# Four edits to a two-layer transformer trunk: priority for the closings, remainder products last, epsilon on VectorE, both token blocks in one cast

## The chip, the core and the metric

The program runs on one core of a Trainium2 chip. The metric is the device time of one launch, in microseconds (us), as the median of three runs. Shares of the span are not the metric; they only help to find where the time is spent.

## What is computed

The reference is a trunk of two post-norm layers over 256 tokens of width 1024, float32. Layer 0 mixes tokens by causal softmax attention with 16 heads of 64, layer 1 by differential attention with 8 heads of 2 x 64; each mixer is followed by a squared-ReLU MLP of width 4096. Every sub-layer is modulated by vectors that come from a conditioning vector c and is closed by a LayerNorm:

```python
h = x * (1 + scale1) + shift1
y = mixer(h)                                    # moba_attention or diff_attention
x = layer_norm(ALPHA * x + (1 + gate1) * y, ln_g[i, 0], ln_b[i, 0])
h = x * (1 + scale2) + shift2
y = square(relu(h @ w_up[i])) @ w_down[i]
x = layer_norm(ALPHA * x + (1 + gate2) * y, ln_g[i, 1], ln_b[i, 1])
```

The modulation vectors are silu(c) @ ada_w + ada_b, six of 1024 for each layer. A LayerNorm divides by the root of its variance plus 1e-5, and differential attention has an RMS norm for each head with the same epsilon.

## The kernel before

**Tiles.** The 256 tokens are two blocks (b = 0, 1) of 128 partitions. Every product is made in float32 precision out of three rounded products: each operand is split into a rounded part `hi` (ScalarE casts it) and a remainder `lo` (VectorE subtracts), and TensorE adds hi x hi, hi x lo and lo x hi in one PSUM bank (`mm3`, L165 to L169, called by `dense`, L171; `dense2`, L176, is the form with two banks for products of width 1024). Weights come by DMA from SyncE's queue into three `raw` buffers and are split in pieces of 128 x 1024 (`split_piece`, L127: cast at L130, subtraction at L131) into 8 `hi` and 8 `lo` buffers. A product of one block with 512 columns and depth 1024 takes 24 matmuls and four such pieces.

**The first pass** (L494 to L541) makes the first columns of V, Q and K of layer 0. For each of 8 depth steps j it loads two blocks of ada_w and reduces them against silu(c) on VectorE (L216, names `aw`) to the scale and shift column `ab`, adds 1 to the scale (L499), loads 1536 columns of weights and splits them, transposes the tokens of both blocks, modulates both at once on ScalarE (L518), and then casts and subtracts block by block (L521, L522). 18 matmuls follow.

**The order of the work** after that is the list `PROGRAM` (L45): V and Q are products, T transposes, S, P, F attention, O the output product, B a boundary (waits for its gate vector, spreads it over the partitions), C a closing, U and X the up product and its transposes, D the down product, Y up products of both blocks together, E the last one. `f` takes steps from a queue of fillers: the other modulation vectors (L216 again, its tile named `aw`, loads in two buffers) and the residuals (L331, L332). In each layer C00 and C10 close the mixer, C01 and C11 the MLP.

**A closing** (`close`, L592) runs `layer_norm` (L280): on VectorE the gate times the accumulator (L289), the residual (L292), the statistics (L302) and their aggregate (L303); then `rsqrt_eps` (L276), on GpSimd, adds epsilon (L277) and raises to the power -0.5 (L278); VectorE normalizes the first half (L308) and makes the bias of the second (L310), which ScalarE normalizes (L311). `modulate` (L314) transposes on TensorE (L320), scales on ScalarE (L324), casts (L327) and subtracts on VectorE (L328) into the tiles `hT` that the next V or U product reads. The last closing (A is None, L594) writes the output and has no `modulate`. Differential attention calls `rsqrt_eps` too (L467), on the sums of L465, ahead of L468.

**Who sets each engine's order.** The instructions of an engine run in a fixed order that is made when the program is built: a list scheduler steps through an estimate of the execution and, whenever an engine comes free there, gives it the most urgent of the instructions that are ready. Urgency is the order in which the program was written; `tc.high_priority()` puts what stands in its block ahead. SyncE's queue, which issues the loads, is ordered in the same way.

```python
def rsqrt_eps(dst, src):
    pool_e.tensor_scalar(out=dst, in0=src, scalar1=EPS, scalar2=None, op0=ALU.add)
    pool_e.tensor_tensor(out=dst, in0=dst, in1=nhalf.to_broadcast(list(src.shape)), op=ALU.pow)
```

Of the kernel before, what the change touches and what calls it, by code (L numbers as in the profile page):

```python
# [16 lines left out]
F32 = mybir.dt.float32  # L17
F32R = mybir.dt.float32r
AF = mybir.ActivationFunctionType
ALU = mybir.AluOpType  # L20
AX = mybir.AxisListType

P = 128
D = 1024
S = 256
KC = D // P
# [6 lines left out]
EPS = 1e-5  # L33
# [33 lines left out]
SHIFT1, SCALE1, GATE1, SHIFT2, SCALE2, GATE2 = range(6)  # L67
# [5 lines left out]
def tile_trunk(ctx: ExitStack, tc: tile.TileContext, x, c, moba_w_in, moba_w_out, diff_w_in, diff_w_out,  # L73
               lam_q1, lam_k1, lam_q2, lam_k2, subln_g, ada_wt, ada_b, ln_g, ln_b, w_up, w_down, cst, out):
    nc = tc.nc
    vec, act, pe, pool_e, sp = nc.vector, nc.scalar, nc.tensor, nc.gpsimd, nc.sync
# [4 lines left out]
    ap_ = ctx.enter_context(tc.tile_pool(name="acts", bufs=1))  # L81
# [83 lines left out]
    def mm3(dst, lhs, rhs, start, stop):  # L165
        (xh, xl), (wh, wl) = lhs, rhs
        pe.matmul(dst, lhsT=xh, rhs=wh, start=start, stop=False)  # L167
        pe.matmul(dst, lhsT=xh, rhs=wl, start=False, stop=False)  # L168
        pe.matmul(dst, lhsT=xl, rhs=wh, start=False, stop=stop)  # L169

    def dense(dst, lhs, rhs):  # L171
        n = len(lhs)
        for k in range(n):
            mm3(dst, lhs[k], rhs[k], k == 0, k == n - 1)

    def dense2(dsts, lhs, rows, start, stop):  # L176

# [11 lines left out]
    tabT = cpool.tile([P, P], F32, name="tabT")  # L189
# [68 lines left out]
    def halves(t, b):  # L258

        return t[:, :, b * P:(b + 1) * P], t[:, :, (2 + b) * P:(3 + b) * P]  # L260
# [4 lines left out]
    def block_ops(tiles, b):  # L265
        return as_ops([halves(t, b) for t in tiles])
# [7 lines left out]
        return t  # L274

    def rsqrt_eps(dst, src):  # L276
        pool_e.tensor_scalar(out=dst, in0=src, scalar1=EPS, scalar2=None, op0=ALU.add)  # L277
        pool_e.tensor_tensor(out=dst, in0=dst, in1=nhalf.to_broadcast(list(src.shape)), op=ALU.pow)  # L278

    def layer_norm(b, accs, gate, parts=None):  # L280
# [33 lines left out]
    def modulate(b, z, A, B, tiles):  # L314
        for h in range(2):
            hi, lo = halves(tiles[h], b)
            ps = psum("tp")
            full = ap_.tile([P, 512], F32, tag="full", name="full", bufs=2)
            for k in range(4):
                pe.transpose(out=ps[:, k * P:(k + 1) * P], in_=z[:, (h * 4 + k) * P:(h * 4 + k + 1) * P], identity=ident)  # L320
            for k in range(4):
                j = h * 4 + k
                ks = slice(k * P, (k + 1) * P)
                act.activation(out=full[:, ks], in_=ps[:, ks], func=AF.Identity, scale=A[:, j:j + 1],  # L324
                               bias=B[:, j:j + 1])
            f3 = full.rearrange("p (k t) -> p k t", t=P)
            act.copy(out=hi, in_=f3)  # L327
            vec.tensor_tensor(out=lo, in0=f3, in1=hi, op=ALU.subtract)  # L328
# [161 lines left out]
    hT0 = act_tiles()  # L490
# [3 lines left out]
    def first_operand(j):  # L494

        ab = small.tile([P, 2], F32, tag="ab0", name="ab0", bufs=3)
        ada_rows(0, SCALE1, j, ab[:, 0:1], "bc", 3)
        ada_rows(0, SHIFT1, j, ab[:, 1:2], "aw", 2)
        vec.tensor_scalar(out=ab[:, 0:1], in0=ab[:, 0:1], scalar1=1.0, scalar2=None, op0=ALU.add)  # L499
        def load_x(cols):  # L500
            for b in range(2):
                sp.dma_start(out=xt[b][:, cols], in_=x[0, b * P:(b + 1) * P, cols])

        if j == 0:
            load_x(slice(0, 256))
        raw = raw_tile()
        wr = moba_w_in[0][j * P:(j + 1) * P, :]
        sp.dma_start(out=raw[:, 0:512], in_=wr[:, 2 * D:2 * D + 512])
        for s_ in range(2):
            sp.dma_start(out=raw[:, 512:1536].rearrange("p (g s n) -> p s g n", g=2, s=2)[:, s_],  # L510
                         in_=wr[:, s_ * D:s_ * D + 512].rearrange("p (g n) -> p g n", n=256))
        if j == 1:
            load_x(slice(256, D))
        tp = psum("tp")
        for b in range(2):
            pe.transpose(out=tp[:, b * P:(b + 1) * P], in_=xt[b][:, j * P:(j + 1) * P], identity=ident)
        full = ap_.tile([P, 512], F32, tag="full", name="full", bufs=2)
        act.activation(out=full[:, :256], in_=tp[:, :256], func=AF.Identity, scale=ab[:, 0:1], bias=ab[:, 1:2])  # L518
        for b in range(2):
            hi, lo = halves(hT0[j // 4], b)  # L520
            act.copy(out=hi[:, j % 4, :], in_=full[:, b * P:(b + 1) * P])  # L521
            vec.tensor_tensor(out=lo[:, j % 4, :], in0=full[:, b * P:(b + 1) * P], in1=hi[:, j % 4, :], op=ALU.subtract)  # L522
        h1, l1 = split_piece(raw[:, 0:1024])
        h2, l2 = split_piece(raw[:, 1024:1536], 512)
        return [(h1[:, 0:512], l1[:, 0:512]), (h1[:, 512:1024], l1[:, 512:1024]), (h2[:, 0:512], l2[:, 0:512])]
# [8 lines left out]
    tps = psum("tp")  # L534
    pe.transpose(out=tps[:, 0:P], in_=t1, identity=ident)
    vec.tensor_copy(out=tabT, in_=tps[:, 0:P])
    ws = first_operand(0)
    for j in range(KC):
        wn = first_operand(j + 1) if j + 1 < KC else None
# [29 lines left out]
        queue_vector(*key)  # L569


    def unit(w, hT):
        ps = psum("mm")
        dense(ps, hT, w)
        return ps

    def out_proj(dsts, g2, b, rows):
# [14 lines left out]
    def close(l, i, b, accs, bd, tiles):  # L592
        A, B, gate, gb, bb = bd
        if A is None:  # L594
            parts = ((0, 512), (512, 1024))
            z, mv, rs = layer_norm(b, accs, gate, parts)
            for c0, c1 in parts:
                vec.scalar_tensor_tensor(out=z[:, c0:c1], in0=z[:, c0:c1], scalar=mv[:, 0:1], in1=gb[:, c0:c1],
                                         op0=ALU.subtract, op1=ALU.mult)
            for c0, c1 in parts:  # L600
                vec.scalar_tensor_tensor(out=z[:, c0:c1], in0=z[:, c0:c1], scalar=rs, in1=bb[:, c0:c1],
                                         op0=ALU.mult, op1=ALU.add)
                sp.dma_start(out=out[0, b * P:(b + 1) * P, c0:c1], in_=z[:, c0:c1])
            return
        z = layer_norm(b, accs, gate)
        modulate(b, z, A, B, tiles)
        filler.appendleft(lambda: residual(b, z, gb, bb))

    def run(program, st):
# [9 lines left out]
    def step_v(st, b, g2):  # L619
        l = st["l"]  # L620
        if l == 0 and g2 == 0:
            ps = kacc[b][0]
        else:
            w = step_load(st, ("wv", l, g2), lambda: load_cols(w_ins[l], v_cols(g2)))
            ps = unit(w, block_ops(st["x"], b))
        evict_v(b, g2, ps)

    def step_qk(st, b, g):
# [25 lines left out]
    def step_up(st, b, j):  # L654
        l = st["l"]
        w = step_load(st, ("wu", l, j), lambda: load_cols(w_up[l], [(j * 512, 512)]))
        ps = psum("mm")
        dense(ps, block_ops(st["x"], b), w)
        r = ap_.tile([P, 512], F32, tag="nat", name="nat", bufs=3)
        act.activation(out=r, in_=ps, func=AF.Relu)  # L660
        act.activation(out=r, in_=r, func=AF.Square)
        st["r", b, j] = r
# [75 lines left out]
    st = {"x": hT0}  # L738
# [48 lines left out]
```

## Time and profile before

| | |
|---|---|
| runs, us | 645.58, 642.77, 645.11 (median 645.11) |
| the profiled execution, us | 644.11, its span 640.7 |
| TensorE busy, share of the span | 609.0 us, 95% |
| VectorE, ScalarE, GpSimd busy | 500.4, 377.6, 22.2 us |
| DMA | 158.23 MB, mean 247 GB/s |

The span goes from the first to the last instruction; the time of the execution also has what lies around it. TensorE's busy time is not its peak, since matmuls are pipelined; so the gaps in it count, and who ended them.

### The profile page before, as it was taken

Reading aid. Unit: us, or ns where it says so; the run is one execution under the profiler, and the core shown is the slowest. Engines: PE = TensorE matmul, PEld = TensorE weight load, DVE = VectorE, ACT = ScalarE, POOL = GpSimd, SP = SyncE. Lnnn points to the kernel's source line nnn. Section 1 sums busy time; section 2 is a strip of 40 time slices with the busy share of each in tenths; the row PEclk is TensorE's granted clock in tenths of the full one; section 3 lists DMA queues with packets and bytes.
Section 4 is the critical chain, followed back from the end, with each engine's and each line's share of the span. In section 5 each row is a group of like instructions: output and inputs, shape, how many; then the busy total and the mean of one; then the engine's idle time right before and its main releaser. Section 6 shows DMA issues by size and latency. Waiting matters only on the chain.

```text
span 640.7 us, 8768 instructions
## 1 busy us (share of the span) xinstructions
PE 609.0 (95%) x3140; PEld 499.6 (78%) x3140; DVE 500.4 (78%) x903; ACT 377.6 (59%) x699; POOL 22.2 (3%) x37
## 2 busy tenths in 40 slices
PE   4889999998999999999999999989999999999994
PEld 3667887886888888888877787767788888888883
DVE  5798998889978878888799989977984646465446
ACT  3448665657846545664477676765775556475530
POOL 0000000001000000000000010021100000000002
PEclk9999999999999999999999999999999999999998
DMA  8997998876689888989765967682663764746401
GB/s 292 406 322 279 313 325 286 288 250 227 215 309 343 308 313 330 326 294 338 268 231 188 337 229 263 232 289 68 208 218 109 259 225 143 255 133 213 182 0 66
DMA packets 65941, 158.23 MB, mean 247 GB/s; under 512 B 4041, under 2 KB 21098, under 8 KB 65898
## 3 DMA queue, kind: packets, MB, share of 16 engines
q1 hardware_dynamic: 65898, 157.68, 70.1%
q8 instruction: 24, 0.39, 0.2%
q14 instruction: 19, 0.16, 0.1%
HBM read 156.62 MB, written 1.05 MB: 246 GB/s over the span
## 4 chain that ended last, share of the span: by engine, by line
PE 64%; DVE 18%; DMA 6%; ACT 4%; issue 3%; POOL 2%; SPq 1%; DVEq 0%; POOLq 0%; ACTq 0%
PE ac L184 13%; PE sc L184 10%; PE mm L687 7%; PE tp L687 6%; DMA aw<-in_ada_w_dram 6%; DVE lo L131 5%; DVE aw L216 4%; PE mm L167 4%; PE mm L169 4%; PE mm L168 4%; PE mm L692 3%; PE tp L692 3%; ACT hi L130 2%; DVE z L292 1%; DVE z L289 1%
## 5 line engine op out<-in xcount | busy, mean ns | idle before, releaser
L131 DVE TENSOR_TENSOR lo<-raw,hi 128x1024 fp32r<-128x1024 f32 x196 | 232.0, 1197 | 44.1 <-ACT hi L130 40.4
L130 ACT CAST hi<-raw 128x1024 fp32r<-128x1024 f32 x196 | 201.3, 1034 | 62.5 <-PE sc L184 43.6
L216 DVE CUSTOM_DVE_ANT_0 aw<-aw,sbc,tabT 128x1024 f32<-128x1024 f32 x96 | 122.0, 1280 | 23.1 <-DMA aw<-in_ada_w_dram 22.7
L167 PE MATMUL mm<-hi,hT 128*128 128x512 f32 x224 | 90.6, 405 | 6.1 <-ACT hi L130 3.2
L169 PE MATMUL mm<-hi,hT 128*128 128x512 f32 x224 | 89.0, 398 | 0.0
L168 PE MATMUL mm<-lo,hT 128*128 128x512 f32 x224 | 88.6, 396 | 0.2 <-DVE lo L131 0.2
L687 PE MATMUL mm<-hT,hi 128*128 128x512 f32 x192 | 60.4, 396 | 0.0
L687 PE MATMUL tp<-hT,hi 128*128 128x512 f32 x192 | 60.3, 395 | 0.0
L167 PEld LDWEIGHTS mm<-hi,hT 128*128 128x128 f32 x224 | 42.3, 189 | 16.1 <-ACT hi L130 3.8
L184 PE MATMUL ac<-hi,sTh 128*128 128x512 f32 x160 | 51.2, 397 | 0.0
L184 PE MATMUL ac<-lo,sTh 128*128 128x512 f32 x160 | 50.8, 394 | 0.0
L184 PE MATMUL ac<-hi,sTl 128*128 128x512 f32 x160 | 50.4, 392 | 0.0
L169 PEld LDWEIGHTS mm<-hi,hT 128*128 128x128 f32 x224 | 42.3, 189 | 9.1 <-DVE hT L328 0.4
L168 PEld LDWEIGHTS mm<-lo,hT 128*128 128x128 f32 x224 | 42.3, 189 | 8.6 <-DVE lo L131 0.3
L184 PE MATMUL sc<-hi,sTh 128*128 128x512 f32 x144 | 45.3, 392 | 0.0
L184 PE MATMUL sc<-lo,sTh 128*128 128x512 f32 x144 | 45.1, 391 | 0.0
L184 PE MATMUL sc<-hi,sTl 128*128 128x512 f32 x144 | 44.6, 390 | 0.0
L692 PEld LDWEIGHTS tp<-hT,lo 128*128 128x128 f32 x192 | 34.4, 188 | 7.5
L692 PEld LDWEIGHTS mm<-hT,lo 128*128 128x128 f32 x192 | 34.4, 188 | 7.3
L697 ACT COPY nat<-mm 128x256 f32<-128x256 f32 x24 | 7.8, 376 | 52.4 <-PE mm L687 52.4
L692 PE MATMUL tp<-hT,lo 128*128 128x256 f32 x192 | 36.0, 279 | 0.0
L692 PE MATMUL mm<-hT,lo 128*128 128x256 f32 x192 | 35.9, 279 | 0.0
(153 smaller groups left out, 899.4 us busy)
## 6 DMA issues: line engine op xcount, KB each, us to landing
aw<-in_ada_w_dram SPq DMA_DIRECT2D x96, 512.0 KB, 5.5
raw<-in_mlp_w_up_dram SPq DMA_DIRECT2D x32, 1024.0 KB, 5.9
raw<-in_mlp_w_down_dram SPq DMA_DIRECT2D x32, 1024.0 KB, 5.1
raw<-in_diff_w_in_dram SPq DMA_DIRECT2D x16, 512.0 KB, 5.1
raw<-in_moba_w_in_dram SPq DMA_DIRECT2D x24, 256.0 KB, 5.5
raw<-in_moba_w_in_dram SPq DMA_DIRECT2D x8, 512.0 KB, 4.8
raw<-in_moba_w_out_dram SPq DMA_DIRECT2D x4, 1024.0 KB, 8.4
raw<-in_diff_w_in_dram SPq DMA_DIRECT2D x4, 1024.0 KB, 5.7
```

The costliest lines, as they stand in the source:

```text
L130: act.copy(out=hi[:, :n], in_=raw_ap)
L131: vec.tensor_tensor(out=lo[:, :n], in0=raw_ap, in1=hi[:, :n], op=ALU.subtract)
L167: pe.matmul(dst, lhsT=xh, rhs=wh, start=start, stop=False)
L168: pe.matmul(dst, lhsT=xh, rhs=wl, start=False, stop=False)
L169: pe.matmul(dst, lhsT=xl, rhs=wh, start=False, stop=stop)
L184: pe.matmul(dsts[h], lhsT=a, rhs=w[:, h * 512:(h + 1) * 512], start=start and k == 0 and i == 0, stop=stop and k == n - 1 and i == 2)
L216: vec.tensor_tensor_reduce(out=aw, in0=aw, in1=sbc, scale=1.0, scalar=adab_cols(l, v)[:, j:j + 1], op0=ALU.mult, op1=ALU.add, accum_out=dst)
L289: vec.tensor_tensor(out=z[:, c_], in0=accs[c_.start // 512][:, a0:a0 + c_.stop - c_.start], in1=gate[:, c_], op=ALU.mult)
L292: vec.scalar_tensor_tensor(out=z[:, c_], in0=xt[b][:, c_], scalar=ALPHA, in1=z[:, c_], op0=ALU.mult, op1=ALU.add)
L687: pe.matmul(ps, lhsT=w[k][0][:, c_], rhs=x3[k], start=first, stop=last)
L692: pe.matmul(ps[:, 0:S], lhsT=w[k][1][:, c_], rhs=x3[k][:, 0:S], start=False, stop=False)
L697: act.copy(out=r[:, i * S:(i + 1) * S], in_=ps[:, S:2 * S])
```

## The change

Four edits. `dense` gets a second order, `late`, in which the products with the left operand's remainder come last; it is used for the V products with g2 = 0 and the U products with j = 0. The addition of epsilon goes from GpSimd to VectorE. In the first pass both blocks are cast in one operation and subtracted in one, and the 1 that was added to the scale column in each step is added once to the table it starts from. The closings but the last get high priority.

```diff
-    def dense(dst, lhs, rhs):
+    def dense(dst, lhs, rhs, late=False):
         n = len(lhs)
+        if not late:
+            for k in range(n):
+                mm3(dst, lhs[k], rhs[k], k == 0, k == n - 1)
+            return
         for k in range(n):
-            mm3(dst, lhs[k], rhs[k], k == 0, k == n - 1)
+            for i in range(2):
+                pe.matmul(dst, lhsT=lhs[k][0], rhs=rhs[k][i], start=k == 0 and i == 0, stop=False)
+        for k in range(n):
+            pe.matmul(dst, lhsT=lhs[k][1], rhs=rhs[k][0], start=False, stop=k == n - 1)
...
     def rsqrt_eps(dst, src):
-        pool_e.tensor_scalar(out=dst, in0=src, scalar1=EPS, scalar2=None, op0=ALU.add)
+        vec.tensor_scalar(out=dst, in0=src, scalar1=EPS, scalar2=None, op0=ALU.add)
         pool_e.tensor_tensor(out=dst, in0=dst, in1=nhalf.to_broadcast(list(src.shape)), op=ALU.pow)
...
-        vec.tensor_scalar(out=ab[:, 0:1], in0=ab[:, 0:1], scalar1=1.0, scalar2=None, op0=ALU.add)
...
-        act.activation(out=full[:, :256], in_=tp[:, :256], func=AF.Identity, scale=ab[:, 0:1], bias=ab[:, 1:2])
-        for b in range(2):
-            hi, lo = halves(hT0[j // 4], b)
-            act.copy(out=hi[:, j % 4, :], in_=full[:, b * P:(b + 1) * P])
-            vec.tensor_tensor(out=lo[:, j % 4, :], in0=full[:, b * P:(b + 1) * P], in1=hi[:, j % 4, :], op=ALU.subtract)
+        act.activation(out=full, in_=tp[:, :2 * P], func=AF.Identity, scale=ab[:, 0:1], bias=ab[:, 1:2])
+        both = hT0[j // 4][:, j % 4, :]
+        act.copy(out=both[:, 0:2 * P], in_=full)
+        vec.tensor_tensor(out=both[:, 2 * P:], in0=full, in1=both[:, 0:2 * P], op=ALU.subtract)
...
+    o = SCALE1 * KC
+    vec.tensor_scalar(out=tabT[:, o:o + KC], in0=tabT[:, o:o + KC], scalar1=1.0, scalar2=None, op0=ALU.add)
...
-        z = layer_norm(b, accs, gate)
-        modulate(b, z, A, B, tiles)
+        with tc.high_priority():
+            z = layer_norm(b, accs, gate)
+            modulate(b, z, A, B, tiles)
...
-            ps = unit(w, block_ops(st["x"], b))
+            ps = unit(w, block_ops(st["x"], b), late=g2 == 0)
...
-        dense(ps, block_ops(st["x"], b), w)
+        dense(ps, block_ops(st["x"], b), w, late=j == 0)
```

## Rows read from the trace of the kernel before

**Rows 1.** Window of one MLP: its length; busy of PE, PEld, DVE, ACT, POOL; clock; DMA share, GB/s.

```profile
185.00:300.00 115.00, 115.00 (x581) 97.71 (x580) 97.61 (x133) 67.51 (x94) 0.00 (x0) 1.00 0.89 314
```

**Rows 2.** Timeline of TensorE at closings: start, us; last: idle before and who ended it.

```profile
145.27 0.63 PE L320 MATMUL tp<-cs,z 128*128 128x128 f32 x4 [0.96 <-DVE nm L310]
148.40 0.50 PE L167 MATMUL mm<-hi,hT 128*128 128x512 f32 x1 [1.13 <-ACT hT L327]
...
459.85 0.66 PE L320 MATMUL tp<-cs,z 128*128 128x128 f32 x4 [0.51 <-DVE z L308]
```

**Rows 3.** Windows of the first pass, columns as in rows 1.

```profile
24.00:34.00 10.00, 8.70 (x38) 6.34 (x36) 8.38 (x14) 3.48 (x7) 0.00 (x0) 1.00 1.05 404
38.79:43.56 4.77, 4.59 (x22) 3.58 (x21) 4.70 (x10) 2.52 (x5) 0.00 (x0) 1.00 1.03 385
```

**Rows 4.** Timeline of VectorE in the first pass, one depth step.

```profile
34.02 0.15 DVE L499 TENSOR_SCALAR ab<-ab 128x1 f32<-128x1 f32 x1
34.08 1.98 DVE L131 TENSOR_TENSOR lo<-raw,hi 128x1024 fp32r<-128x1024 f32 x2
35.98 0.48 DVE L522 TENSOR_TENSOR hT<-full,hT 128x128 fp32r<-128x128 f32 x2
36.38 1.28 DVE L216 CUSTOM_DVE_ANT_0 aw<-aw,sbc,tabT 128x1024 f32<-128x1024 f32 x1
```

**Rows 5.** Timeline of VectorE in differential attention, behind the RMS norm.

```profile
420.05 0.42 DVE L468 TENSOR_TENSOR on<-mm,ss 128x256 f32<-128x256 f32 x1 [0.90 <-POOL ss L278]
420.39 0.15 DVE L439 RECIPROCAL sums<-sums 128x2 f32<-128x2 f32 x1
```

**Rows 6.** Timeline of VectorE in layer 0's C00.

```profile
135.98 1.28 DVE L216 CUSTOM_DVE_ANT_0 aw<-aw,sbc,tabT 128x1024 f32<-128x1024 f32 x1 [0.46 <-DMA aw<-in_ada_w_dram]
...
140.19 1.21 DVE L131 TENSOR_TENSOR lo<-raw,hi 128x1024 fp32r<-128x1024 f32 x1
141.32 1.28 DVE L216 CUSTOM_DVE_ANT_0 aw<-aw,sbc,tabT 128x1024 f32<-128x1024 f32 x1
...
142.52 0.20 DVE L303 BATCH_NORM_AGGREGATE bna<-bns 128x2 f32<-128x12 f32 x1
142.64 1.17 DVE L131 TENSOR_TENSOR lo<-raw,hi 128x1024 fp32r<-128x1024 f32 x1
...
144.58 0.55 DVE L308 TENSOR_SCALAR z<-z,bna,rs 128x512 f32<-128x512 f32 x1 [0.69 <-POOL rs L278]
```

**Rows 7.** SyncE's queue and ScalarE's casts around layer 0's first up products.

```profile
134.34 8.62 SPq L215 DMA_DIRECT2D aw<-in_ada_w_dram  x3
143.84 0.38 SPq L145 DMA_DIRECT2D raw<-in_mlp_w_up_dram  x1
166.02 1.06 ACT L130 CAST hi<-raw 128x1024 fp32r<-128x1024 f32 x1 [0.30 <-PE mm L169]
```

**Rows 8.** Timeline of GpSimd.

```profile
142.81 1.08 POOL L277 TENSOR_SCALAR rs<-bna 128x1 f32<-128x1 f32 x1 [142.00 <-DVE bna L303]
143.97 0.57 POOL L278 TENSOR_TENSOR rs<-rs,nhalf 128x1 f32<-128x1 f32 x1
...
426.89 0.22 POOL L277 TENSOR_SCALAR ss<-ss 128x2 f32<-128x2 f32 x1 [6.88 <-ACT sq L465]
...
626.20 0.93 POOL L278 TENSOR_TENSOR rs<-rs,nhalf 128x1 f32<-128x1 f32 x1
```

**Rows 9.** Timeline of VectorE at the last closings.

```profile
625.28 1.42 DVE L598 SCALAR_TENSOR_TENSOR z<-z,bna,bc 128x512 f32<-128x512 f32 x2
...
634.11 0.26 DVE L303 BATCH_NORM_AGGREGATE bna<-bns 128x2 f32<-128x24 f32 x1
634.41 1.41 DVE L598 SCALAR_TENSOR_TENSOR z<-z,bna,bc 128x512 f32<-128x512 f32 x2
636.28 1.41 DVE L601 SCALAR_TENSOR_TENSOR z<-z,rs,bc 128x512 f32<-128x512 f32 x2 [0.46 <-POOL rs L278]
```

**Rows 10.** Chain that ended last, one down product: start, us, what.

```profile
190.74 5.45 PE sc L184 x24
```

More of the change, by code (lines that the diff above doesn't have):

```diff
@@ L516, in first_operand @@
             pe.transpose(out=tp[:, b * P:(b + 1) * P], in_=xt[b][:, j * P:(j + 1) * P], identity=ident)
-        full = ap_.tile([P, 512], F32, tag="full", name="full", bufs=2)
-        act.activation(out=full[:, :256], in_=tp[:, :256], func=AF.Identity, scale=ab[:, 0:1], bias=ab[:, 1:2])
-        for b in range(2):
-            hi, lo = halves(hT0[j // 4], b)
-            act.copy(out=hi[:, j % 4, :], in_=full[:, b * P:(b + 1) * P])
-            vec.tensor_tensor(out=lo[:, j % 4, :], in0=full[:, b * P:(b + 1) * P], in1=hi[:, j % 4, :], op=ALU.subtract)
+        full = ap_.tile([P, 2 * P], F32, tag="full", name="full", bufs=2)
+        act.activation(out=full, in_=tp[:, :2 * P], func=AF.Identity, scale=ab[:, 0:1], bias=ab[:, 1:2])
+        both = hT0[j // 4][:, j % 4, :]
+        act.copy(out=both[:, 0:2 * P], in_=full)
+        vec.tensor_tensor(out=both[:, 2 * P:], in0=full, in1=both[:, 0:2 * P], op=ALU.subtract)
         h1, l1 = split_piece(raw[:, 0:1024])
@@ L569, in tile_trunk, with unit @@
         queue_vector(*key)
-    def unit(w, hT):
+    def unit(w, hT, late=False):
         ps = psum("mm")
-        dense(ps, hT, w)
+        dense(ps, hT, w, late)
         return ps
```

## The prediction

> **What bounds the kernel now.** I read the windows by stage first, then TensorE's timeline for its gaps, then, at each gap, the queue that ended it. In the long MLP stage TensorE is busy all of 115 us [rows 1]: no edit can win there, since all of them leave the number of matmuls as it is. What can be won or lost lies in the gaps elsewhere. Seven stand in the four closings that are followed by a product [rows 2]: in layer 0's C00 TensorE idles 0.96 us ahead of the transposes and 1.13 us ahead of the first up product, and at the five other transposes 0.40 to 0.52 us each (the last is the row at 459.85). The reader is to see who ended them: the normalization, or the cast of hT, and in none of them the subtraction that makes hT's remainder. The first pass is another case. VectorE runs there without a pause, 4.70 of 4.77 us in a step [rows 3], and so sets the pace, with the DMA queues full beside it.
>
> **The sum** is made against the profiled execution, 644.11 us (span 640.7, and 3.4 around it), which is 1.0 below the median of 645.11; I carry the difference over to the median.
>
> **First pass.** A step of VectorE is 0.06 for L499, 1.90 for two subtractions of weights, 0.40 for two of tokens and 2.41 for two reductions, from start to start [rows 3, 4]. L499 goes. One subtraction of 128 x 256 takes 0.34 from start to start, by one of that shape [rows 5], in place of 0.40. That is 0.12 us less in each of the five steps in which VectorE never pauses: -0.6. In the earlier steps, which wait for the chain through L499, I take -0.1 more. The 1 that is added to the table costs one small operation, 0.15 at most (L499's own time), ahead of a first reduction that is waiting for its load; the joint cast gives block 0 its operand a little later and block 1 its own earlier, and TensorE has 0.2 us of idle in such a step to take that up. Taken: -0.7. The bound on one side is the DMA: a step at 385 GB/s moves 1.84 MB, which takes 4.55 us at the 404 GB/s of the stretch before [rows 3], so no step can fall below that, -0.22 each, or -1.1. On the other side, if loads already set the pace, it is 0.
>
> **Priority.** In C00, between the halves of L289, a reduction of a filler waits 0.46 us for its load and then runs 1.2 us, until 137.19; another runs from 141.32 to 142.52, between statistics and aggregate [rows 6]. Both were written earlier in the program and so were more urgent; now the closing passes them. The subtraction at 140.19 stays, I think: it got in because the aggregate was not yet ready when VectorE came free, and priority chooses only among what is ready. So the chain of C00 is 0.46 + 1.2 + 1.2 = 2.9 us shorter. TensorE cannot win all that, since the product of block 1 fills most of it: what is to be had are the gaps of 1.13 and 0.96 [rows 2]. The first goes whole; the second falls to the size of the other five, a saving of 0.5: -1.6. In the other closings what stands between the steps are subtractions for later products, which got in because they were ready, so priority changes little there: 0.
>
> What priority moves back are the two reductions, and with them their buffers. SyncE's queue spent 8.62 us on three loads for such reductions, and the load of up weights stood behind them until 143.84 [rows 7]. If reductions come 2.9 us later and the queue keeps its order, those weights do too. Bounds for priority: -2.1 (both gaps whole) to +1.3 (2.9 less the 1.6). I take -1.6, since the queue's order is made anew and a load of weights that is ready passes one that is not.
>
> **Epsilon.** GpSimd's addition took 1.08 us in C00 and 0.22 in attention where VectorE was idle [rows 8]; beside the first ran a subtraction of two SBUF tiles from 142.64 [rows 6], and it ended with it. The power took 0.57 with VectorE idle, and 0.93 where L598, which reads two SBUF tiles too, ran until 626.70; it ended 0.43 later [rows 8, 9]. From the aggregate to L308 the chain is now 144.58 - 142.52 = 2.06 us [rows 6]. After the change the addition takes 0.15 (L499), VectorE goes on with a subtraction of 1.13, and the power starts some 0.2 later. If that subtraction holds it up, it ends 1.13 + 0.43 behind the addition, and L308 comes after 0.1 + 0.1 + 1.13 + 0.43 = 1.8: -0.25 for each closing. If it does not, L308 comes when the subtraction is over, -0.7, more than each gap holds. If a further subtraction gets in between aggregate and addition, as one did ahead of the aggregate, the chain is 0.9 longer. I take the first, since both rows with two inputs on VectorE show GpSimd waiting: five gaps by 0.25, -1.2; bounds -2.3 (the gaps whole) and +4.5 (five times 0.9, with nothing beside it).
>
> The Trainium skill, SBUF — State Buffer, Who interferes with whom, speaks against the edit: a VectorE instruction with two SBUF inputs and a GpSimd instruction that reads SBUF exclude each other, and the second to come waits for the whole first. By that rule moving the addition does not end the wait but hands it to the power; the rows at 142.81 and 626.20 agree, and the sum without it would have -2.3 in place of -1.2.
>
> At the end of the kernel the same chain is bare: aggregate at 634.11, L601 at 636.28 [rows 9]. VectorE has two L598 of 0.7 in between, which end at 635.8, some 0.1 later with the addition ahead of them. L601 then comes between 635.9 and, if the power waits for both, 636.4: taken -0.2, bounds -0.4 and +0.1.
>
> In differential attention there are eight such norms, and VectorE waited 0.90 behind one [rows 5]. The addition now stands in VectorE's queue, where a reduction or a subtraction of 1.2 us may be ahead of it; on GpSimd that same operation held it up too. I take 0, with -0.3 each as the one bound (the 0.22, and the 0.08 from one GpSimd operation to the next [rows 8], go) and +1.2 each as the other.
>
> **Remainders last.** No gap is ended by the remainder of hT, so nothing is won: 0. The cost is in buffers. The second block's product now keeps the rounded pieces of its weights until its 18th, 20th, 22nd and 24th matmul, not its 6th, 12th, 18th and 24th. At 5.45 / 24 = 0.227 us a matmul [rows 10] that is 2.7, 1.8, 0.9 and 0 us later, and ScalarE's casts follow just those releases [rows 7]. Behind that product stands another of 24 matmuls whose weights are there, 5.45 us of cover; four pieces at 1.2 us, the first cast 1.4 us before the product ends, need some 3.5. Covered, with 2 us to spare; without cover it would be +2.7 at each of three places.
>
> **Sum:** -0.7 - 1.6 - 1.2 - 0.2 = -3.7 us, that is 640.4 for the profiled execution and **641.4** for the median. The measurement can tell about 0.5%, 3.2 us, from no change.
>
> **Rivals.** *The power is not held up* and attention wins too: -0.7 - 2.1 - 2.3 - 0.4 - 2.4 = -7.9, 637.2. For it speaks that the power never ran beside a long subtraction in this trace; against it the 0.93. Chance 0.13. *Priority and epsilon change nothing that TensorE sees:* a list scheduler that takes what is ready still lets subtractions in, a further one stands ahead of the addition, and the five gaps stay; what is left is C00 with its weights a little late, -1.0, and half of the first pass, -0.4: 643.7. For it speaks the subtraction at 140.19, which got in without any urgency [rows 6]. Chance 0.25. *The addition queues on VectorE in attention*, and the time gets longer: each of eight norms waits up to 1.2 us for a reduction that itself may be waiting for its load, as at 135.98 [rows 6], and everything behind the norm is late by as much. With 0.9 on average that is +7.2 - 3.7 = +3.5, 648.6; it decides the sign once TensorE sees more than 3.7 / 8 = 0.46 of each wait. Against it: GpSimd's addition suffered from the same operations. Chance 0.14.
>
> **How the numbers follow.** Forecast 0.48, rivals 0.13, 0.25 and 0.14. The forecast's own range is 638.5 to 643.5; two thirds of it (0.32) lie beyond 3.2 us. Faster: 0.32 + 0.13 = 0.45; slower by over 0.5%: 0.11 of the last rival; the rest, 0.44, within. The range takes in the first rival's time nearly and half of the last rival: 636.0 to 647.0.
>
> **What would show it.** Right: steps of 4.65 us in the first pass; no reduction inside C00's chain, and no idle ahead of its first up product; from aggregate to L308 about 1.8 us, the power at 1 us or more beside a subtraction; L601 0.2 nearer to the last aggregate. Wrong: steps still at 4.77; subtractions in front of the addition; TensorE waiting for weights behind a `late` product, or for the norm's transposes in attention by more than now.

## The result: half a per cent slower

The changed kernel takes 646.46 us (median of 18 runs, 642.70 to 653.17), the kernel before 642.75 beside it (18 runs, 641.44 to 645.58): a ratio of 1.0055, interval 1.0038 to 1.0072, or 3.7 us more, where 3.7 less was forecast. The sign is wrong. The forecast's base, 645.11, was the median of three runs; of 18 it is 642.75. That the time still lies in the range is luck: the range's upper end was drawn for a rival that did not happen, additions queueing in attention. The profiled execution took 646.26 us with a span of 644.5, 3.8 longer than before.

To see where, take the same matmul in both traces and subtract its starts (after minus before). Where its place among the matmuls moved by more than one, the row says so; one matmul more or less ahead of it is 0.227 us.

| matmul, before to after (us) | shift | what lies ahead of it |
|---|---|---|
| 12.39 to 13.30 | +0.9 | start |
| 52.76 to 53.95 | +1.2 | first pass |
| 73.18 to 74.30 | +1.1 | layer 0's attention opens |
| 96.51 to 98.68 | +2.2 | layer 0's attention |
| 139.16 to 142.71 | +3.6 | its end |
| 161.25 to 163.06 | +1.8 | C00, C10 |
| 315.85 to 317.66 | +1.8 | MLP of layer 0 |
| 339.36 to 341.08 | +1.7, with 6 matmuls fewer ahead of it: +3.1 at equal work | C01, C11 |
| 359.09 to 363.95 | +4.9, with 3 matmuls more ahead of it: +4.2 at equal work | layer 1's first V and Q products |
| 390.62 to 395.08 | +4.5 | layer 1's attention |
| 469.79 to 474.08 | +4.3 | its end, C00, C10 |
| 631.44 to 635.70 | +4.3 | MLP of layer 1 |

The last closings give 0.5 back. So 1.2 is lost in the first pass, 2.4 in layer 0's attention, where no line was edited, 1.8 won in C00 and C10, 1.3 lost in C01 and C11, and some 1.2 behind them, 0.83 of it in one pause.

### The profile page after: what moved, and what is told of

It is laid out like the page before. It is cut to its first block, busy times and chain, and to the rows that moved or that the text cites. A ratio compares the mean times of both kernels' runs of the same rounds, so it can differ in the third digit from the quotient of the medians.

```text
span 644.5 us, 8746 instructions
## 1 busy us (share of the span) xinstructions
PE 612.4 (95%) x3140; PEld 500.5 (78%) x3140; DVE 499.4 (77%) x904; ACT 375.6 (58%) x691; POOL 18.0 (3%) x21
## 4 chain that ended last, share of the span: by engine, by line
PE 63%; DVE 17%; DMA 12%; issue 3%; ACT 3%; POOL 2%; SPq 1%; DVEq 0%; ACTq 0%; POOLq 0%
PE ac L192 14%; PE sc L192 10%; DMA aw<-in_ada_w_dram 10%; PE mm L697 7%; PE tp L697 6%; DVE lo L131 5%; DVE aw L224 5%; PE mm L702 3%; PE tp L702 3%; PE mm L169 3%; PE mm L167 3%; PE mm L168 3%; PE mm L180 2%; PE sc L425 1%; POOL rs L286 1%
## 5 line engine op out<-in xcount | busy, mean ns | idle before, releaser
L167 PE MATMUL mm<-hi,hT 128*128 128x512 f32 x176 | 71.5, 407 | 5.4 <-ACT hi L130 3.9
L168 PE MATMUL mm<-lo,hT 128*128 128x512 f32 x176 | 70.6, 401 | 0.0
L169 PE MATMUL mm<-hi,hT 128*128 128x512 f32 x176 | 70.1, 398 | 0.0
L167 PEld LDWEIGHTS mm<-hi,hT 128*128 128x128 f32 x176 | 33.3, 190 | 13.7 <-ACT hi L130 4.5
L169 PEld LDWEIGHTS mm<-hi,hT 128*128 128x128 f32 x176 | 33.4, 190 | 6.8
L168 PEld LDWEIGHTS mm<-lo,hT 128*128 128x128 f32 x176 | 33.4, 190 | 6.3
```

## The profile after

**The page** (busy time and first line of the chain) says only that TensorE's busy time grew (609.0 us before, the same 95%) and that loads stand more often on the path: DMA is 12% of the chain that ended last, 6% before.

```profile
PE 612.4 (95%) x3140; PEld 500.5 (78%) x3140; DVE 499.4 (77%) x904; ACT 375.6 (58%) x691; POOL 18.0 (3%) x21
```

**First pass**, windows and VectorE's timeline, to set against [rows 3, 4]. The steady step is 4.64 us (37.78 to 42.42) in place of 4.77, as forecast:

```profile
24.00:34.00 10.00, 7.95 (x35) 5.91 (x34) 7.60 (x11) 4.96 (x8) 0.00 (x0) 1.00 1.04 399
37.78:42.42 4.64, 4.64 (x22) 3.58 (x21) 4.58 (x8) 1.66 (x4) 0.00 (x0) 1.00 0.88 295
```

```profile
6.11 0.17 DVE L545 TENSOR_SCALAR tabT<-tabT 128x8 f32<-128x8 f32 x1
8.11 1.28 DVE L224 CUSTOM_DVE_ANT_0 aw<-aw,sbc,tabT 128x1024 f32<-128x1024 f32 x1 [1.83 <-DMA aw<-in_ada_w_dram]
...
40.19 1.98 DVE L131 TENSOR_TENSOR lo<-raw,hi 128x1024 fp32r<-128x1024 f32 x2
42.09 0.42 DVE L529 TENSOR_TENSOR hT<-full,hT 128x256 fp32r<-128x256 f32 x1
42.42 1.28 DVE L224 CUSTOM_DVE_ANT_0 aw<-aw,sbc,tabT 128x1024 f32<-128x1024 f32 x1
```

But the first reduction waits until 8.11; before it began at 6.18. It is now the shift's, whose load was issued second: the 1 goes into the part of the table that the scale's reduction reads, and the scheduler put the other one first. The shift is 0.9 at the first product, 1.7 by 23.55, and 1.2 when the steady steps have won some back.

**Layer 0's attention.** TensorE, then VectorE, ahead of the last q and k transposes:

```profile
120.75 0.63 PE L374 MATMUL tp<-cs,nat 128*128 128x128 f32 x4 [1.66 <-DVE nat L367]
```

```profile
117.45 1.28 DVE L224 CUSTOM_DVE_ANT_0 aw<-aw,sbc,tabT 128x1024 f32<-128x1024 f32 x1 [0.42 <-DMA aw<-in_ada_w_dram]
...
119.19 1.22 DVE L131 TENSOR_TENSOR lo<-raw,hi 128x1024 fp32r<-128x1024 f32 x1
120.32 0.29 DVE L367 TENSOR_TENSOR nat<-nat,rtmp 128x128 f32<-128x128 f32 x1
```

TensorE waits 1.66 us for the rotation of q and k (L364 to L367), which stands behind a reduction that waits for its load and then behind a subtraction. The order differs from that of before much further back, in SyncE's queue, here before and after the change:

```profile
68.28 0.34 SPq L215 DMA_DIRECT2D aw<-in_ada_w_dram  x1
68.72 0.38 SPq L145 DMA_DIRECT2D raw<-in_moba_w_in_dram  x1
70.55 0.34 SPq L215 DMA_DIRECT2D aw<-in_ada_w_dram  x1
70.94 0.43 SPq L145 DMA_DIRECT2D raw<-in_moba_w_in_dram  x1
```

```profile
69.17 2.74 SPq L223 DMA_DIRECT2D aw<-in_ada_w_dram  x2
72.01 0.94 SPq L145 DMA_DIRECT2D raw<-in_moba_w_in_dram  x2
```

Before, a load for a reduction and one of weights take turns. After, two loads for reductions stand together; the second waits for its buffer, 2.74 us in all, with the weights behind it.

**C00.** TensorE and VectorE, to set against [rows 2, 6]:

```profile
146.88 0.63 PE L328 MATMUL tp<-cs,z 128*128 128x128 f32 x4 [0.38 <-DVE nm L318]
...
150.17 0.50 PE L180 MATMUL mm<-hi,hT 128*128 128x512 f32 x1
```

```profile
141.98 1.27 DVE L224 CUSTOM_DVE_ANT_0 aw<-aw,sbc,tabT 128x1024 f32<-128x1024 f32 x1
...
143.17 0.20 DVE L311 BATCH_NORM_AGGREGATE bna<-bns 128x2 f32<-128x12 f32 x1
143.29 1.17 DVE L131 TENSOR_TENSOR lo<-raw,hi 128x1024 fp32r<-128x1024 f32 x1
144.38 0.15 DVE L285 TENSOR_SCALAR rs<-bna 128x1 f32<-128x1 f32 x1
...
144.52 1.22 DVE L131 TENSOR_TENSOR lo<-raw,hi 128x1024 fp32r<-128x1024 f32 x1
146.19 0.55 DVE L316 TENSOR_SCALAR z<-z,bna,rs 128x512 f32<-128x512 f32 x1 [0.45 <-POOL rs L286]
```

The idle of 1.13 ahead of the first up product is gone, the 0.96 is 0.38: the gaps shrank as the forecast said. But they shrink in the run with the first pass's edit alone too (below), so this trace does not show that priority did it. Only one of the two reductions left the chain; the one at 141.98 still stands ahead of the aggregate. And epsilon's addition (L285) does not follow the aggregate at once: a subtraction gets in first, so the way from aggregate to normalization (L316) is 3.02 us, not 1.8. In the six closings with a product behind them it is 3.0, 2.4, 2.9, 2.4, 2.7 and 2.4, against 2.06 in each before.

GpSimd's power beside that subtraction, and in the last closing, where VectorE's L607 holds it up; then VectorE there, to set against [rows 8, 9]:

```profile
144.68 1.47 POOL L286 TENSOR_TENSOR rs<-rs,nhalf 128x1 f32<-128x1 f32 x1 [143.85 <-DVE B L255]
...
638.97 0.92 POOL L286 TENSOR_TENSOR rs<-rs,nhalf 128x1 f32<-128x1 f32 x1 [8.20 <-DVE rs L285]
```

```profile
638.37 0.26 DVE L311 BATCH_NORM_AGGREGATE bna<-bns 128x2 f32<-128x24 f32 x1
638.67 0.15 DVE L285 TENSOR_SCALAR rs<-bna 128x1 f32<-128x1 f32 x1
...
640.06 1.41 DVE L610 SCALAR_TENSOR_TENSOR z<-z,rs,bc 128x512 f32<-128x512 f32 x2
```

The power is held up, 1.47 us beside the subtraction in place of 0.57; in the last closing its 0.92 is what it was before [rows 8]. At the end nothing gets in, and the way is 1.69 where it was 2.17 [rows 9].

**C01 and layer 1's first products.** TensorE ahead of the transposes of C01 before, and then, after the change, there and at the second transposes of q and k:

```profile
326.40 0.63 PE L320 MATMUL tp<-cs,z 128*128 128x128 f32 x4 [0.42 <-DVE nm L310]
```

```profile
330.64 0.63 PE L328 MATMUL tp<-cs,z 128*128 128x128 f32 x4 [1.72 <-DVE nm L318]
...
363.95 0.63 PE L374 MATMUL tp<-cs,nat 128*128 128x128 f32 x4 [0.83 <-DVE nat L367]
```

C01's closing stands on VectorE behind a reduction whose load lands later: the closing starts at 322.29 in place of 318.92, 3.4 us later, where TensorE is only 1.8 behind. Neither priority nor epsilon is needed for that: the runs with the first pass's edit alone and with the remainders last alone have pauses of 1.83 and 1.77 us there. Behind the `late` V product ScalarE idles 3.59 us, until 350.71, for the transposes of q and k, which stand behind 16 of its matmuls; counted by the n-th matmul, TensorE loses nothing there until 359.

## Experiments: each part alone

Every ratio is to the kernel before on the same chip; each kernel was timed in five rounds.

**The first pass alone** (the diff's hunks at the first pass and the table):

```diff
-        vec.tensor_scalar(out=ab[:, 0:1], in0=ab[:, 0:1], scalar1=1.0, ...)
+    vec.tensor_scalar(out=tabT[:, o:o + KC], in0=tabT[:, o:o + KC], scalar1=1.0, ...)
+        act.copy(out=both[:, 0:2 * P], in_=full)
+        vec.tensor_tensor(out=both[:, 2 * P:], in0=full, in1=both[:, 0:2 * P], op=ALU.subtract)
```

> The kernel before with the first pass's edit alone: the joint cast and split of both blocks' tokens, and the 1 added to the table. Theory (the order of the work is remade): the step of VectorE in the first pass is 4.65 us and wins 0.7 there, as forecast, but with fewer instructions in the first pass the scheduler puts layer 0's attention in another order, and TensorE loses there the 2.4 us that the changed kernel lost; together +1.7, a ratio of 1.0026. Rival (the attention of layer 0 was lost through another part of the change, or by chance): -0.7 and nothing else, 0.999.

647.26 us, 1.0070 (1.0043 to 1.0097). The theory's place is right, its size too small: +1.3 by 52 us, +3.8 by 136 us, with a pause ahead of the same transposes at 121.01. This part alone loses as much as the whole change. In C00, where nothing was edited, it wins 1.35 back: the idle of 0.96 is 0.64, that of 1.13 ahead of the first up product is gone:

```profile
147.38 0.63 PE L320 MATMUL tp<-cs,z 128*128 128x128 f32 x4 [0.64 <-DVE nm L310]
```

So this part and priority go for the same gaps.

**Priority alone:**

```diff
+        with tc.high_priority():
             z = layer_norm(b, accs, gate)
             modulate(b, z, A, B, tiles)
```

> The kernel before with the priority of the closings alone. Theory: both reductions leave C00's chain, the idle ahead of its first up product goes, and nothing else moves: -1.7 us, a ratio of 0.9974. Rival: the weights of the up projections come later because the reductions do, and the win is given back in C00 itself or in the products behind it: between -0.3 and +0.5, 1.000.

651.40 us, 1.0127 (1.0100 to 1.0154). Both fell. TensorE, then VectorE, in C00 and C10:

```profile
152.59 0.79 PE L169 MATMUL mm<-hi,hT 128*128 128x512 f32 x1 [3.10 <-DVE hT L328]
```

```profile
148.26 1.28 DVE L289 TENSOR_TENSOR z<-sc,gate 128x512 f32<-128x512 f32 x2
...
151.86 0.68 DVE L328 TENSOR_TENSOR hT<-full,hT 128x512 fp32r<-128x512 f32 x1
```

And VectorE at that place before:

```profile
147.38 1.28 DVE L289 TENSOR_TENSOR z<-sc,gate 128x512 f32<-128x512 f32 x2
148.57 0.68 DVE L328 TENSOR_TENSOR hT<-full,hT 128x512 fp32r<-128x512 f32 x1
149.18 1.29 DVE L292 SCALAR_TENSOR_TENSOR z<-x,z 128x512 f32<-128x512 f32 x2
```

Before, the remainders of block 0 (L328) go between the steps of block 1's closing. With priority that closing runs through, the remainder comes at 151.86 in place of 148.57, and the third matmul of the product wants it. Behind the pause TensorE's granted clock falls: its window is

```profile
150.00:155.00 5.00, 1.64 (x4) 0.92 (x5) 4.22 (x10) 2.12 (x4) 1.12 (x2) 0.73 0.83 302
```

where 0.50 would be the lower level, 1.2 GHz, throughout. C00 and C10 make 5.0 of the 9.2 us by which this span is longer; 1.4 are lost ahead of them and 2.8 behind the MLP of layer 0, and the cause of those stays open.

**Epsilon alone:**

```diff
-        pool_e.tensor_scalar(out=dst, in0=src, scalar1=EPS, scalar2=None, op0=ALU.add)
+        vec.tensor_scalar(out=dst, in0=src, scalar1=EPS, scalar2=None, op0=ALU.add)
```

> The kernel before with epsilon on VectorE alone. Theory (the changed kernel's loss lies elsewhere): the chain from aggregate to L308 is some 0.3 us shorter in the closings, the attention norms win or lose nothing: -0.5 us, between -1.2 and 0, a ratio of 0.999. Rival (the addition queues on VectorE, in attention above all): the eight norms of layer 1 wait 0.4 us each, +3 us, 1.005, and this part alone explains the loss.

647.47 us, 1.0065 (1.0042 to 1.0088). The rival's number, but not by its mechanism: VectorE's idle time behind the attention norms fell from 6.4 us to 4.8. The way from aggregate to L308 is 3.01 us in C00 and C10 and 2.93 in the others, with a subtraction ahead of the addition in all six. And the loss lies in the closings: the shift of the same matmul is +0.5 at 139.16, +2.0 at 161.25 and at 315.85, +3.4 at 359.09, +2.3 at 447.25 and +4.9 at 469.79. In C00 the idle ahead of the first up product grew from 1.13,

```profile
149.33 0.50 PE L167 MATMUL mm<-hi,hT 128*128 128x512 f32 x1 [1.60 <-ACT hT L327]
```

and the granted clock was 0.66 from 150 to 155 us.

**Remainders last alone:**

```diff
-            ps = unit(w, block_ops(st["x"], b))
+            ps = unit(w, block_ops(st["x"], b), late=g2 == 0)
-        dense(ps, block_ops(st["x"], b), w)
+        dense(ps, block_ops(st["x"], b), w, late=j == 0)
```

> The kernel before with the remainders last alone (the late products: the first up unit of each layer and layer 1's first V unit). Theory: the rounded pieces of V's weights are kept until late, ScalarE's casts of the next weights start some 4 us later, and TensorE loses 2.5 us between layer 1's first V product and its first scores; the up units lose nothing or little: +2.5 us, a ratio of 1.004, and this is the larger part of the change's loss. Rival (forecast): the cover holds, 0.0 us, 1.000, and the 2.5 us come from another part.

643.69 us, 0.9997 (0.9973 to 1.0020). The theory fell. By itself this part costs nothing, as forecast.

So the parts don't add up: by their ratios 4.5, 8.2, 4.2 and -0.2 us, 17 in all, and together they cost 3.7. Some parts must be mending others.

## Experiments: which parts belong together

**The change without the first pass's edit** (that hunk undone):

```diff
-        act.copy(out=both[:, 0:2 * P], in_=full)
+            act.copy(out=hi[:, j % 4, :], in_=full[:, b * P:(b + 1) * P])
```

> The changed kernel with the first pass as before (priority, epsilon and remainders last stay). Theory (the first pass's edit remakes the order of layer 0's attention and of its own start, and that is what the whole change loses): 642.0 us, a ratio of 0.998 to the kernel before. Rival (the closings lose too: from aggregate to the normalization 2.4 to 3.0 us in place of 2.06, and layer 1's first V product behind it): 645 to 646, a ratio of 1.003 or more.

642.28 us, 0.9983 (0.9957 to 1.0009): the theory. The first pass's edit costs the whole change some 4 us.

**The same without remainders last**, so priority and epsilon alone:

```diff
-        dense(ps, block_ops(st["x"], b), w, late=j == 0)
+        dense(ps, block_ops(st["x"], b), w)
```

> The changed kernel without the first pass's edit and without any remainders last (priority and epsilon stay). Theory: the wait of 3.1 us for the remainder in C00 and the half clock behind it are there as in the run with priority alone, and epsilon on VectorE does not change that: +6 to +8 us, a ratio of 1.010. Rival (the forecast: no gap is ended by the remainder, the order of the products is worth nothing): as the run with it, 642.3, 0.998.

653.54 us, 1.0149 (1.0110 to 1.0189): the theory, and more than it. TensorE waits 3.40 us for the remainder in C00 (149.82), and its matmuls stand 3.63 apart at the same place in C01 (338.93). With remainders last, the same place is

```profile
150.60 2.11 PE L182 MATMUL mm<-hi,hT 128*128 128x512 f32 x8 [0.19 <-DVE hT L336]
```

0.19 us of waiting. So beside priority and epsilon this part is worth some 11 us (653.54 to 642.28), and without them nothing.

**Remainders last in the up products only:**

```diff
-            ps = unit(w, block_ops(st["x"], b), late=g2 == 0)
+            ps = unit(w, block_ops(st["x"], b))
```

> The changed kernel without the first pass's edit and with the remainders last in the up products alone, not in layer 1's V product. Theory: the V product, which keeps its rounded pieces and so holds up the casts of the weights behind it, cost 2.3 us between 347 and 366 us in the run with both; without it 640.3, a ratio of 0.995. Rival (V's product needs it as C00's does, since the closings ahead of it have priority too): a pause for the remainder of hT behind C01 or C11, 644 or more.

644.82 us, 1.0030 (1.0003 to 1.0057): the rival. V's product behind C01 needs it too:

```profile
332.08 0.50 PE L169 MATMUL mm<-hi,hT 128*128 128x512 f32 x1 [3.22 <-DVE hT L336]
```

The 2.3 us between 347 and 366 that the theory wanted back were read off transposes that had moved behind other products. Counted by the n-th matmul, the run with both `late` products loses nothing between 345 and 359, and 1.8 from there to 391; this run loses 0.1 there. So keeping the rounded pieces may cost something behind 359 after all; these are single profiles, and it stays open.

**Priority and remainders last, nothing else:**

```diff
+        with tc.high_priority():
+            ps = unit(w, block_ops(st["x"], b), late=g2 == 0)
+        dense(ps, block_ops(st["x"], b), w, late=j == 0)
```

> The kernel before with priority and remainders last, and nothing else. Priority alone cost 8 us, of which TensorE's wait for the remainder of hT in C00 was 3.1 and the half clock behind it some 3.4. Theory: with the remainders last that wait has 16 matmuls, 3.6 us, in front of it and is gone, the clock stays up, and the win of C00 is left: -1.5 us, a ratio of 0.998. Rival (priority loses elsewhere too: the weights of the up projection are late because the reductions are): +2 or more, 1.003.

645.12 us, 1.0050 (1.0024 to 1.0076): the rival's number. Its profiled execution, 642.99, is the fastest of its twelve; in it no wait for the remainder is left in C00, and 2.2 us are lost between 359 and 391. What the slower ones lose its trace cannot show. With epsilon on VectorE added, this kernel is the one of 642.28 us, on the same chip and with an interval clear of this one: beside these two parts epsilon wins (2.8 us by the medians, 4.3 by the ratios), where alone it costs 4.2. Why stays open.

## Experiments: what in the first pass costs 4 us

**The joint cast and split, the 1 added in each step as before** (against the first pass's edit alone):

```diff
+        vec.tensor_scalar(out=ab[:, 0:1], in0=ab[:, 0:1], scalar1=1.0, ...)
-    vec.tensor_scalar(out=tabT[:, o:o + KC], in0=tabT[:, o:o + KC], scalar1=1.0, ...)
```

> The kernel before with the joint cast and split of the tokens alone; the 1 is added in each step as before. Theory: the start is as before (first reduction near 6.2 us), but the fewer operations of the joint cast are what remakes the order of layer 0's attention, so TensorE loses there some 2 us between 60 and 130 us: +1.7, a ratio of 1.003. Rival (the attention's new order comes from the removed additions, not from the joint cast): -0.5, 0.999.

648.12 us, 1.0078 (1.0046 to 1.0110). The theory, with a larger loss: the first reduction is at 6.23, but there are pauses of 1.25 and 2.13 us near 107 and 122.

**ScalarE's joint cast alone**, two subtractions:

```diff
-            act.copy(out=hi[:, j % 4, :], in_=full[:, b * P:(b + 1) * P])
+        act.copy(out=both[:, 0:2 * P], in_=full[:, :256])
```

> The kernel before with ScalarE's joint cast alone: one cast of 128 x 256 in place of two of 128 x 128; the two subtractions and the addition in each step stay. Theory: this cast is what remakes the order of SyncE's loads in layer 0's attention (two loads for reductions stand together, ahead of weights), though it is the part that the forecast counted at nothing: +3 to +4.5 us, a ratio of 1.005 to 1.007, with a pause of TensorE of 1.5 us or more ahead of the last q and k transposes near 121 us. Rival (the order is remade by the joint subtraction): 0.0 us.

647.96 us, 1.0080 (1.0056 to 1.0104): the theory, above its size. Two loads for reductions stand together (69.17 us), and the pause is 1.33 us at 120.30.

**The joint split and the table, two casts, shift first:**

```diff
-        ada_rows(0, SCALE1, j, ab[:, 0:1], "bc", 3)
         ada_rows(0, SHIFT1, j, ab[:, 1:2], "aw", 2)
+        ada_rows(0, SCALE1, j, ab[:, 0:1], "bc", 3)
+        for b in range(2):
+            act.copy(out=both[:, b * P:(b + 1) * P], in_=full[:, b * P:(b + 1) * P])
+        vec.tensor_tensor(out=both[:, 2 * P:], in0=full[:, :256], in1=both[:, 0:2 * P], op=ALU.subtract)
```

> The kernel before with the rest of the first pass's edit: the joint subtraction and the 1 in the table, but two casts as before, and the shift's load first. Theory: VectorE's step is 4.65 us as forecast, SyncE's order is that of before, so the 0.6 us are won and not given back: -0.6, a ratio of 0.999, and no pause near 121 us. Rival (any edit of the first pass brings the pause): +2 or more.

644.16 us, 1.0016 (0.9992 to 1.0040). Steps of 4.64 us (37.12 to 41.76) and no pause near 121, so the order part holds; the gain of 0.6 is not seen, and the interval would hardly show it.

**The whole change with the shift's load first:**

```diff
-        ada_rows(0, SCALE1, j, ab[:, 0:1], "bc", 3)
         ada_rows(0, SHIFT1, j, ab[:, 1:2], "aw", 2)
+        ada_rows(0, SCALE1, j, ab[:, 0:1], "bc", 3)
```

> The changed kernel with the two loads of each step of the first pass in the other order: the shift's rows before the scale's. In the changed kernel VectorE's first reduction is that of the shift, whose load is second, so it starts at 8.11 in place of 6.18 us. Theory: loads and reductions then have one order again, the first reduction starts near 6.2, and the first product, at 12.71 us, comes 0.9 earlier: 645.5, a ratio of 0.9986 to the changed kernel. Rival (the load was late by chance): no difference, first reduction still near 8.

646.93 us, 1.0062 (1.0033 to 1.0092). The mechanism is right and the time is not:

```profile
6.17 1.28 DVE L224 CUSTOM_DVE_ANT_0 aw<-aw,sbc,tabT 128x1024 f32<-128x1024 f32 x1
...
7.77 1.28 DVE L224 CUSTOM_DVE_ANT_0 aw<-aw,sbc,tabT 128x1024 f32<-128x1024 f32 x1 [0.30 <-DMA aw<-in_ada_w_dram]
```

The start is won, and the shift at 21 us is +0.2 in place of +1.8. By 130 us it is +4.0: the same pause at 119.69 takes it back.

Now the decisive pair. **The joint cast in the last of eight steps alone, and in the first seven alone:**

```diff
+        if j == KC - 1:
+            act.copy(out=both[:, 0:2 * P], in_=full[:, :256])
```

> The kernel before with the joint cast in the last of the first pass's eight steps alone, two subtractions as before. One cast of 128 x 256 in place of two of 128 x 128 is 0.1 us of ScalarE's time. Theory (order): SyncE's loads in layer 0's attention stand in the order that the joint cast of all steps brought, and most of its loss is here: +3 us or more, a ratio of 1.005, with a pause ahead of the q and k transposes near 120 us. Rival (the cast itself, in every step): an eighth of the loss, +0.6 at most, 1.001.

```diff
+        if j < KC - 1:
+            act.copy(out=both[:, 0:2 * P], in_=full[:, :256])
```

> The kernel before with the joint cast in the first seven steps, the last with two casts. Theory (order): SyncE's loads keep the order of before, there is no pause near 120 us, and what is left is the start, where a token activation goes ahead of the cast of weights on ScalarE: +0.5 to +1, a ratio of 1.001. Rival (the cast itself): seven eighths of the loss, +4, 1.007.

The last step alone: 647.94 us, 1.0064 (1.0033 to 1.0094). The first seven: 645.05, 1.0025 (0.9995 to 1.0055). One cast, 0.1 us shorter, costs some 4 us; the two intervals still overlap, and the traces separate them. With it alone SyncE's queue and TensorE are

```profile
67.99 2.60 SPq L215 DMA_DIRECT2D aw<-in_ada_w_dram  x2
70.69 0.94 SPq L145 DMA_DIRECT2D raw<-in_moba_w_in_dram  x2
```

```profile
120.43 0.63 PE L366 MATMUL tp<-cs,nat 128*128 128x128 f32 x4 [2.81 <-DVE nat L359]
```

and then a window of TensorE at a clock of 0.57:

```profile
121.00:125.00 4.00, 3.93 (x28) 3.05 (x26) 3.96 (x6) 1.76 (x3) 0.00 (x0) 0.57 0.89 308
```

With the first seven the loads take turns as before and there is no such pause:

```profile
69.52 0.34 SPq L215 DMA_DIRECT2D aw<-in_ada_w_dram  x1
69.96 0.39 SPq L145 DMA_DIRECT2D raw<-in_moba_w_in_dram  x1
71.79 0.34 SPq L215 DMA_DIRECT2D aw<-in_ada_w_dram  x1
72.18 0.43 SPq L145 DMA_DIRECT2D raw<-in_moba_w_in_dram  x1
```

That kernel's profile loses 1.2 us by 55 us and nothing in attention. It is so in every trace: the six kernels with the joint cast in the last step have the two loads together and a pause of 1.3 to 2.8 us ahead of these transposes, and the fourteen others have neither. Not the cast's own time is the cost, but the order that the scheduler makes behind the last step. VectorE's order there changes together with that of the loads, and which of the two brings the pause was not separated.

**The whole change with the last step as before, and the same with the shift first:**

```diff
+        if j < KC - 1:
+            act.copy(out=both[:, 0:2 * P], in_=full[:, :2 * P])
+        else:
+            act.copy(out=hi[:, j % 4, :], in_=full[:, b * P:(b + 1) * P])
```

> The whole change, but the last step of the first pass cast and split in two operations each, as before. Theory (order): layer 0's attention is that of before, the closings win what they won without the first pass's edit (0.998), and the start loses its 1 us: 643, a ratio of 1.000, 3 to 4 us under the whole change. Rival: as the whole change, 646.5, 1.0055.

> The same, with the shift's load ahead of the scale's in every step, so that the first reduction does not wait for the second load. Theory: the start comes 0.9 earlier than in the run before: 642, a ratio of 0.9985, the best of the versions with all parts. Rival: no difference between the two.

642.54 us, 0.9979 (0.9951 to 1.0007), and 643.44, 0.9996 (0.9968 to 1.0024). The first is the theory: 3.9 us under the whole change from one step of eight. The second shows nothing beyond it. Neither is surely faster than before.

**Epsilon by place**, in the better of these: on VectorE in attention and at the end only, and in the closings only:

```diff
+    def rsqrt_eps(dst, src, on=vec):
+        rsqrt_eps(rs, mv[:, 1:2], pool_e if parts is None else vec)
```

> The whole change with the last step of the first pass as before, and epsilon back on GpSimd in the six closings with a product behind them; on VectorE in the attention norms and the last closings. Theory: the way from aggregate to normalization is 2.06 us again, TensorE's pauses at the transposes are 0.3 to 0.5 shorter each: -1 to -2 us against 642.5, so 641, a ratio of 0.996. Rival (the product behind each closing covers the longer way, and the closing's loss costs nothing): 642.5, 0.998.

```diff
+    def rsqrt_eps(dst, src, on=pool_e):
+        rsqrt_eps(rs, mv[:, 1:2], vec)
```

> The same, with epsilon on VectorE in the closings and back on GpSimd in the eight attention norms. Theory: in attention the addition on VectorE neither wins nor loses (the forecast's 0): 642.5, a ratio of 0.998. Rival (it wins 0.3 in each of eight norms there, which is why the run without any of it was slower): 645, 1.002.

643.59 us, 0.9995 (0.9971 to 1.0019), and 643.64, 0.9980 (0.9953 to 1.0007). In the first the way from aggregate to normalization is 2.06 again (1.53 in C10), and no time is won by it: beside priority and the late remainders, the longer way that epsilon made costs less than these runs can tell, in either place. Alone it cost 4.2, and its trace puts that into the closings; so what the longer way costs depends on what else was changed.

## Why the prediction was wrong

- **First pass, −0.7.** This is the step that failed. The steady step came out at 4.64, as forecast. But the joint cast was costed on TensorE's operands only ("TensorE has 0.2 us of idle in such a step to take that up"), and the work behind the first pass was taken as fixed. It is remade: the part alone measured +4.5 us (1.0070), and the last step's cast alone costs some 4, most of it in attention, up to 70 us later. To this comes 0.9 at the start, where the 1 in the table let the wrong reduction go first; the forecast had 0.15 for it. Another 0.8 goes by 23.55, and the joint cast in the first seven steps alone loses 1.1 there.
- **Priority, −1.6.** Both gaps shrank as foretold in the whole change (1.13 to 0, 0.96 to 0.38), but only one of the two reductions left the chain, and the first pass's edit alone shrinks the same gaps. Without that edit the change still wins 1.6 in C00 and C10, and only because another part covers priority's price. The price was looked for in the loads of up weights. It is +8.2 alone, and the largest part of it comes from the wait for the remainder of hT, overtaken by the other block's closing. "Priority chooses only among what is ready" was the right rule; I did not ask what becomes ready just after the choice.
- **Remainders last, 0.** "No gap is ended by the remainder of hT, so nothing is won" is true of the kernel before (0.9997 alone) and false beside priority, where it is worth some 11 us. The parts were costed one by one against the trace of before. The buffers' price of 2.7 was not seen in that run alone.
- **Epsilon, −1.2 in five closings.** (There are six closings with a product behind them, where the prediction counts four; its five gaps are right.) That the power would be held up behind a subtraction was right: 1.47 us beside one, 0.57 with nothing beside it. The Trainium skill, SBUF — State Buffer, Who interferes with whom, says that a VectorE instruction with two SBUF inputs contends with a GpSimd instruction that reads SBUF; the trace agrees, with these two numbers. Which subtraction was wrong: another one stands ahead of the addition, the case that I had kept as the upper bound, and the way grew from 2.06 to between 2.4 and 3.0. At the end, where −0.2 was taken, it shrank by 0.48.
- **Attention norms, 0.** VectorE's idle behind them went from 6.4 to 5.3 us in the changed kernel, so the rival on the slower side, an addition that queues on VectorE, did not happen. The kernel came out slower by a way that no rival had.

## What to carry to other kernels

Where a list scheduler writes the order, an edit's largest cost can lie in stages that it doesn't touch: ask what order comes out, DMA queues first, and try each part both alone and taken away. Two parts can each look worthless or harmful and be a pair; here priority without the late remainders costs 8 us and the remainders without priority win nothing. And when you compare two traces by one matmul, count what stands ahead of it: a product that moved looks like time lost. A gain of 0.1 us per step is not worth a new order.

## What the runs showed beside

One order does not give one time. The last kernel (epsilon in closings) and the one with the last step as before have the same order on all engines up to layer 1's attention, and the same order of loads to the end. Ahead of C01 SyncE's queue and TensorE's transposes read, in the one and then the other:

```profile
309.10 7.28 SPq L223 DMA_DIRECT2D aw<-in_ada_w_dram  x3
```

```profile
325.49 0.63 PE L328 MATMUL tp<-cs,z 128*128 128x128 f32 x4 [0.23 <-DVE nm L318]
```

```profile
311.84 7.83 SPq L223 DMA_DIRECT2D aw<-in_ada_w_dram  x3
```

```profile
328.80 1.09 PE L328 MATMUL tp<-cs,z 128*128 128x128 f32 x4 [3.07 <-DVE nm L318]
```

```profile
328.50:332.00 3.50, 3.20 (x12) 2.73 (x13) 3.50 (x5) 2.33 (x5) 0.00 (x0) 0.51 0.98 312
```

Loads that end some 3 us later keep VectorE's reductions, the closing behind them and then TensorE waiting, 3.07 us in place of 0.23, and the clock goes to its lower level for what follows. The 4 us between the fastest and the slowest runs of the kernel before are of this size, so a single profile can be told from another only where the same wait stands in several kernels, as the pause near 121 us does.
